# A hybrid attention layer: two attention items scored among the query products, reciprocals on GpSimd, two merge tiles among the last items, merge weights split two steps ahead

## The chip, the cores and the metric

The kernel runs on one core of one Trainium2 chip. The metric is the device time of one execution in microseconds, as a median of several runs. The engines are named as in the profile: PE is TensorE (PEld its weight loads), DVE is VectorE, ACT is ScalarE, POOL is GpSimd, and SP issues the transfers (DMAs).

## What is computed

One layer of a transformer trunk over 1024 latent tokens on a grid of 16 x 64 and 256 context tokens, width 1024: a half-step SwiGLU, two token mixers on the same normalised input, their merge, and a second half-step SwiGLU. The change lies between the projections and the merge:

```python
o_na = _neighbourhood_attention(qa, ka, va, cka, cva, rpb[l], n_rows)   # 8 heads of 64: 8 x 16 window + 256 context keys
q_mla = _mla_q(qn, _axial_rope(qr, ang_r, ang_c))                       # 8 heads of 64 + 32
o_mla = _blocked_attention(q_mla, k_mla, v_mla)                         # all 1280 keys
y = (ga * (o_na @ w_o_na) + gb * (o_mla @ w_o_mla)) @ w_out             # the merge
```

Both attentions are a softmax over the keys: scores, maximum, exponential, sum, and the product with the values divided by the sum.

## The kernel before, in words

All matrices are float32. For precision an operand is split into a high part (an ACT cast to the matmul's reduced format, `fp32r`) and a low part (a DVE subtraction); `mm3` makes three matmuls of two split operands, `weigh` two. Tiles are 128 rows high.

The order of work before the attention is written out by hand in a `Plan`: a list of main steps, with side steps set to run after given main steps by `spread`. The last steps are the products for the keys and values (`kv_heads`) and for the queries (`q_heads(0)`, `q_heads(1)`, nine steps each; the first four of these make the rotated parts, the next four the wide products). Matmuls and transfers keep the order in which they are written; transfers all go through SP's queue, which is worked in order, and a transfer waits there until its buffer is free. Stores of the plan are put off by two or three steps (`store`).

The attention is then a loop over 64 items: 32 of neighbourhood attention (8 heads, 4 column blocks `j` each) and 32 of latent attention (8 heads, 4 blocks of 256 queries). An item has three kinds of work:

- `scores`: matmuls into PSUM banks of the kind `s`; DVE takes the scores out (with the bias, in `L1840`), and finds the maximum (`L1814`, `L1847`). For a neighbourhood item this comes in two halves.
- the steps in the list `soft`: two or four exponentials with their sums on ACT (`L1849`, `L1948`), then the reciprocal of the sums on DVE (`L1851`, `L1952`), and for every second item `widen`, in which POOL spreads the reciprocals of two items over a tile (`L1806`).
- `values`: three or five parts. Each transposes a piece of the probabilities on PE, casts it (ACT) and subtracts (DVE), and returns a closure that multiplies it with the values. The last one calls `head_out`, where ACT and DVE take out the result, and POOL multiplies it by the reciprocal and writes high and low parts (`L1792` to `L1795`).

The loop runs the scores three items ahead (`AHEAD`) and the value products two parts behind (`LAG`), and spreads the next items' scores and softmax steps over the parts of the present one. Loads of a head are issued when its first item is scored: six pieces for neighbourhood attention (queries, context keys, keys; first bias; values of two blocks; context values and second bias; values of the others; third bias), in a pool `w` of 12 tiles; the third bias has a pool of its own (`y`). Before the change item 0 is scored amid the last two query products (its tiles in pool `f`); items 1 and 2 are scored, with their softmax steps right behind, between the plan and the loop.

The merge multiplies the two attention outputs (`ona`, `omla`) by two weight matrices in eight tiles `d` of 128 columns. A tile has four steps `wo_step(d, ci, s)`: two halves `ci` of the tokens, for each a product of 12 matmuls with the neighbourhood weights (`s` = 0) and one with the latent weights (`s` = 1). DVE multiplies each by its gate (`z`), adds the two and the sum is split for the output product. The weights of a tile are loaded (`wo_load`), and split in two halves (`wo_split`). The class `FirstMerge` makes the two `s` = 0 products of tile 0 ahead of time: one amid the very last item, one behind it; they use only neighbourhood results, which have long been complete.

Of the kernel before, what the change touches and what calls it, by code (L numbers as in the profile page):

```python
# [8 lines left out]
F32 = mybir.dt.float32  # L9
# [34 lines left out]
def hybrid_block(ctx: ExitStack, tc: tile.TileContext, a: dict, out: bass.AP):  # L44
# [15 lines left out]
    def open_pool(key, name, bufs, side):  # L60
        pools[key] = tc.alloc_tile_pool(name=nm(name), bufs=bufs, side=side, reuse_waits="tile")
# [1516 lines left out]
    class NaHead:  # L1578


        def loads(self, h):
            self.h = h
            i, b = h // 2, (h % 2) * 64
            self.q, self.ql, self.kvc, self.k = q, ql, kvc, k = [W() for _ in range(4)]
            for s in range(2):
                o = 64 * s
                ld(f32(q[o:o + 64, :]), qas[i][0, b:b + 64, :])
                ld(f32(ql[o:o + 64, :]), qas[i][1, b:b + 64, :])
                ld(f32(kvc[o:o + 64, 0:256]), kas[i][s, b:b + 64, NLAT:])
            yield  # L1590
            for s in range(2):
                ld(f32(k[64 * s:64 * s + 64, :]), kas[i][s, b:b + 64, :NLAT])
            self.bias = [W(F32), W(F32)]
            ld(self.bias[0][:, :768], a["bias"][h, 0])
            yield
            self.va = va = W()
            for j in range(2):
                self.values(va, j)
            yield
            ld(f32(kvc[:, 256:512]), vcs[h])  # L1600
            ld(self.bias[1][:, :768], a["bias"][h, 1])
            yield
            self.vb = vb = W()
            for j in range(2, 4):
                self.values(vb, j)
            yield
            self.bias.append(U(F32, "y"))
            ld(self.bias[2][:, :768], a["bias"][h, 2])
            yield
# [123 lines left out]
    plan.spread([lambda d=d: query_cols(0, d) for d in range(6)], o, o + 12)  # L1733
    o = len(plan.main)
    plan.step(*calls(kv_heads(1, ckv[1]), 9))
    plan.spread([lambda d=d: query_cols(1, d) for d in range(6)], o + 3, o + 14)
    plan.step(*calls(q_heads(0, cqn[0]), 9))
    o = len(plan.main)
    plan.step(*calls(q_heads(1, cqn[1]), 9))
    heads = {}  # L1740

    na0 = na_loads(0)

    def weights():
        close_pools("v")
        open_pool("w", "weights", 12, "left")
        open_pool("y", "third", 2, "left")
        open_pool("f", "first", 2, "left")

    def score_banks():  # L1750
        banks[0] = "mv"

    early = []

    def first_scores():
        if not early:
            it = na_item(0, 0)
            started.append(it)
            early.append(it.scores())
        next(early[0], None)  # L1760

    def first_soft():
        while soft:
            soft.pop(0)()

    plan.spread([weights], o - 3, o - 2)
    plan.spread(calls(na0, 6), o - 2, o + 4)
    plan.spread([score_banks], o + 2, o + 3)
    plan.spread([first_scores] * 2, o + 6, o + 8)
    plan.spread([first_soft], o + 8, o + 9)  # L1770

    ona, omla = [], []

# [34 lines left out]
    def sums_of(n):  # L1808
        if n // 2 not in sums:
            sums[n // 2] = ST(4)  # L1810
        return sums[n // 2][:, (n % 2) * 2:(n % 2) * 2 + 2]

    def copy_max(dst, src, m):
        nc.vector.tensor_scalar(dst, src, 1.0, FMIN, op0=ALU.mult, op1=ALU.max, accum_out=m)  # L1814

# [4 lines left out]
    class NaItem:  # L1820
# [3 lines left out]
        def scores(self):  # L1824
            hd, j = self.head, self.j
            kg = hd.k.rearrange("p (r c) -> p r c", c=64)
            cx = PB("s")
            key = "u" if self.n else "f"
            self.pr = pr = [U(key=key), U(key=key)]
            m, n_, l, r = ST(4), ST(2), ST(2), sums_of(self.n)  # L1830
            for s in range(2):
                loc = PB("s")
                o = s * 512 + j * P
                kw = kg[:, 4 * s:4 * s + 12, KSTART[j]:KSTART[j] + 32]
                cs = cx[:, s * 256:(s + 1) * 256]
                mmul(cs, hd.q[:, o:o + P], hd.kvc[:, 0:256], start=True, stop=False)
                mmul(cs, hd.ql[:, o:o + P], hd.kvc[:, 0:256], start=False, stop=True)
                mmul(loc[:, :384], hd.q[:, o:o + P], kw, start=True, stop=False)
                mmul(loc[:, :384], hd.ql[:, o:o + P], kw, start=False, stop=True)
                nc.vector.tensor_tensor_reduce(out=pr[s][:, :384], in0=loc[:, :384],  # L1840
                                               in1=hd.bias[BVAR[j]][:, s * 384:(s + 1) * 384], scale=1.0, scalar=FMIN,
                                               op0=ALU.add, op1=ALU.max, accum_out=m[:, 2 * s:2 * s + 1])
                if s == 0:
                    yield
            for s in range(2):
                copy_max(pr[s][:, 384:640], cx[:, s * 256:(s + 1) * 256], m[:, 2 * s + 1:2 * s + 2])
            nc.vector.tensor_reduce(n_, m.rearrange("p (s c) -> p s c", s=2), axis=AX.X, op=ALU.max, negate=True)  # L1847
            for s in range(2):
                soft.append(lambda s=s: nc.scalar.activation(pr[s][:, :640], pr[s][:, :640], AF.Exp,  # L1849
                                                             bias=n_[:, s:s + 1], accum_out=l[:, s:s + 1]))  # L1850
            soft.append(lambda: nc.vector.reciprocal(r, l))  # L1851
            if self.n % 2:
                soft.append(lambda: widen(self.n))
            yield
# [67 lines left out]
    class MlaItem:  # L1922
# [3 lines left out]
        def scores(self):  # L1926
# [21 lines left out]
                nc.scalar.activation(x, x, AF.Exp, bias=n_[:, s:s + 1], accum_out=l[:, i:i + 1])  # L1948

            def total():  # L1950
                nc.vector.tensor_tensor(r, l[:, 0:2], l[:, 2:4], op=ALU.add)
                nc.vector.reciprocal(r, r)  # L1952

            for s in range(2):
                soft.append(lambda s=s: exp(prl[s], s))
# [53 lines left out]
            for b in range(4):  # L2009
                yield lambda h=h, b=b: mla_item(h, b)  # L2010

    AHEAD = 3
    LAG = 2
    todo = list(items_())
    pending = []
# [21 lines left out]
            started.append(it)  # L2037
            yield from it.scores()

    for n in range(1, AHEAD):  # L2040
        for _ in start(n):
            pass
        while soft:
            soft.pop(0)()
    class FirstMerge:


        def load(self):
            self.r = T2()
            ld(self.r, a["wo"][0][:, 0:512])  # L2050

        def split(self):
            t = W()
            self.w = split_to(t[:, 0:512], t[:, 512:1024], self.r)
            self.pb = [PB("s") for _ in range(2)]

        def step(self, ci, ks):
            open_group[0] = True
            for k in ks:
                mm3(self.pb[ci], [x[:, k * P:(k + 1) * P] for x in self.w],  # L2060
                    [x[:, ci * 512:ci * 512 + 512] for x in ona[k]], k == 0, k == 3)
            open_group[0] = False

    fm = FirstMerge()
    for n in range(len(todo)):
        ahead = start(n + AHEAD)
        if n == len(todo) - 3:
            fm.load()
        if n == len(todo) - 2:
            fm.split()  # L2070
        parts = started[n].values()
        soft_n, soft[:] = list(soft), []
        for x, part in enumerate(parts):
            pending.append(part())
            for _ in range(-(-len(soft_n) // (len(parts) - x))):
                soft_n.pop(0)()
            for _ in range(5 // len(parts)):
                next(ahead, None)
            if n == len(todo) - 1 and x:
                fm.step(0, (x - 1,))  # L2080
            if len(pending) > LAG:
                pending.pop(0)()
        for _ in ahead:
            pass
    for w in pending:
        w()
    fm.step(1, range(4))
    pinned[0] = False

    close_pools("u", "t", "f", "y", "w")  # L2090
# [8 lines left out]
        wos[d] = [load(a["wo"][d])]  # L2099

    def wo_split(d, s):
        wos[d].append(split(wos[d][0][:, s * 512:(s + 1) * 512]))

    def z_load(d):
        for ci in range(2):
# [4 lines left out]
    def wo_step(d, ci, s):  # L2110
        c = slice(ci * 512, ci * 512 + 512)
        if ci + s == 0:
            yt.append(list(zip(*[duo() for _ in range(2)])))
        if d + s == 0:
            pb = fm.pb[ci]
        else:
            pb = PA()
            w = wos[d][1 + s]
            for k in range(4):
                mm3(pb, [x[:, k * P:(k + 1) * P] for x in w], [x[:, c] for x in (ona, omla)[s][k]], k == 0, k == 3)  # L2120
        z = zt[d, ci, s]
        vec.tensor_tensor(z, pb, z, op=ALU.mult)
        if s:
            x = zt[d, ci, 0]
            vec.tensor_tensor(x, x, z, op=ALU.add)
            hi, lo = yt[d]
            split_to(hi[ci], lo[ci], x)

    plan = Plan()
    wo_load(0)  # L2130
    z_load(0)
    wos[0].append(None)
    wo_split(0, 1)
    for d in range(KD):
        o = len(plan.main)
        plan.step(*[lambda d=d, ci=ci, s=s: wo_step(d, ci, s) for ci in range(2) for s in range(2)])
        if d + 1 < KD:
            plan.spread([lambda d=d: (wo_load(d + 1), z_load(d + 1))], o, o + 1)
            plan.spread([lambda d=d, s=s: wo_split(d + 1, s) for s in range(2)], o + 2, o + 4)
    g5row = []  # L2140
    wsets = [Set(a["wout"][e], 512, "ut"[e], "tv"[e]) for e in range(2)]
    plan.spread([lambda: wsets[0].load(0)], len(plan.main) - 8, len(plan.main) - 7)
# [182 lines left out]
```

## Time and profile before

| | us |
|---|---|
| median of three runs | 2590.11 (2586.34 to 2592.45) |
| the profiled execution | 2593.43 |
| its span | 2591.6 |
| query products of the second half of the tokens | until 1349 |
| neighbourhood attention in the loop | 1356 to 1500 |
| latent attention | 1500 to 1764 |
| merge | 1764 to 1855.5 |

The rows of the profile are read like this. A row of the timeline has its start in us from the span's beginning, its length, the engine, the line, the operation, what it writes and reads (`bm`, `bs`, `bv` are PSUM banks; `w` the tiles of heads; `xu`, `xf`, `t` working tiles; `xo` attention outputs; `d` scratch in device memory), shapes, and how many instructions it joins. In brackets stands how long the engine was idle before it, and what ended that wait. A row of the groups has the count, the busy time, the mean in ns, and the idle time before with what ended most of it. A row of the windows has a stretch, its length, the busy time of each engine with its count of instructions, the clock granted to TensorE, the share of the DMA engines' time, and GB/s. `L120`, `L132` and `L158` are helpers, through which most operations pass.

### The profile page before, as it was taken

Reading aid. Unit: us, or ns where it says so; the run is one execution under the profiler, and the core shown is the slowest. Engines: PE = TensorE matmul, PEld = TensorE weight load, DVE = VectorE, ACT = ScalarE, POOL = GpSimd, SP = SyncE. Lnnn points to the kernel's source line nnn. Section 1 sums busy time; section 2 is a strip of 40 time slices with the busy share of each in tenths; the row PEclk is TensorE's granted clock in tenths of the full one; section 3 lists DMA queues with packets and bytes.
Section 4 is the critical chain, followed back from the end, with each engine's and each line's share of the span. In section 5 each row is a group of like instructions: output and inputs, shape, how many; then the busy total and the mean of one; then the engine's idle time right before and its main releaser. Section 6 shows DMA issues by size and latency. Waiting matters only on the chain.

```text
span 2591.6 us, 38557 instructions
## 1 busy us (share of the span) xinstructions
PE 2543.2 (98%) x13289; PEld 2168.0 (84%) x13289; DVE 1884.0 (73%) x3616; ACT 1224.1 (47%) x2334; POOL 220.3 (8%) x365
## 2 busy tenths in 40 slices
PE   7999999999999999999999999999999999999998
PEld 5888888998888788889889999987788888888887
DVE  4689887877577577874559988885535788778557
ACT  4532223445445753343438887782256322323633
POOL 0000000000001100001004422220021000000002
PEclk9999999999999999999999999999999999999999
DMA  7567674877676665767888732215225566556755
GB/s 288 165 215 256 227 247 167 274 266 257 195 246 218 233 207 193 233 217 206 286 255 244 225 82 76 76 46 186 75 106 187 195 235 225 176 195 247 254 194 196
DMA packets 273892, 523.08 MB, mean 202 GB/s; under 512 B 33248, under 2 KB 84256, under 8 KB 273696
## 3 DMA queue, kind: packets, MB, share of 16 engines
q1 hardware_dynamic: 273696, 520.62, 60.1%
q8 instruction: 105, 1.72, 0.3%
q14 instruction: 91, 0.75, 0.1%
HBM read 375.21 MB, written 145.29 MB: 201 GB/s over the span
## 4 chain that ended last, share of the span: by engine, by line
PE 69%; issue 17%; DVE 6%; ACT 5%; DMA 2%; SPq 1%; POOL 0%; DVEq 0%; ACTq 0%; POOLq 0%
PE bm L158 25%; PE bs L158 25%; PE bv L158 15%; PE bm L161 2%; DVE t L120 1%; ACT xu L1948 1%; DVE xu L1814 1%; DMA w<-d 1%; PE bs L161 1%; DVE xu L120 1%; ACT t L1974 1%; ACT xu L120 1%; DVE t L1975 1%; DVE xv L120 1%; ACT t L120 1%
## 5 line engine op out<-in xcount | busy, mean ns | idle before, releaser
L158 PE MATMUL bm<-xu,xu 128*128 128x512 f32 (+1 forms) x2442 | 596.0, 388 | 3.3 <-ACT t L120 2.2
L120 ACT CAST xu<-t 128x512 fp32r<-128x512 f32 x589 | 345.5, 617 | 483.7 <-DVE t L120 329.6
L158 PEld LDWEIGHTS bm<-xu,xu 128*128 128x128 f32 x2442 | 449.9, 188 | 95.7 <-ACT t L120 4.3
L120 DVE TENSOR_TENSOR xu<-t,xu 128x512 fp32r<-128x512 f32 x589 | 382.3, 683 | 140.4 <-ACT xu L120 140.4
L158 PE MATMUL bs<-xu,xu 128*128 128x512 f32 (+2 forms) x1581 | 388.2, 384 | 0.0
L158 PE MATMUL bs<-xv,xu 128*128 128x512 f32 x1488 | 358.1, 390 | 3.1 <-DVE t L120 2.9
L158 PEld LDWEIGHTS bs<-xu,xu 128*128 128x128 f32 x1581 | 291.7, 188 | 58.0
L158 PE MATMUL bv<-xv,xu 128*128 128x512 f32 x1342 | 335.9, 389 | 0.0
L158 PEld LDWEIGHTS bs<-xv,xu 128*128 128x128 f32 x1488 | 278.5, 188 | 63.2 <-issue 5.5
L158 PEld LDWEIGHTS bv<-xv,xu 128*128 128x128 f32 x1342 | 251.5, 188 | 52.1
L120 DVE TENSOR_TENSOR xu<-xu,xu 128x512 fp32r<-128x512 f32 x291 | 195.2, 686 | 98.7 <-ACT xu L120 98.1
L120 DVE TENSOR_TENSOR t<-t,t 128x512 f32<-128x512 f32 (+3 forms) x328 | 211.0, 646 | 12.8 <-ACT t L120 9.6
L158 PE MATMUL bs<-w,w 96*128 96x512 f32 (+3 forms) x832 | 208.8, 369 | 11.1 <-DMA w<-d 5.9
L158 PE MATMUL bv<-xu,xu 128*128 128x512 f32 x722 | 191.5, 389 | 0.0
L120 POOL TENSOR_SCALAR st<-st 128x1 f32<-128x1 f32 x64 | 31.2, 487 | 1659.0 <-ACT t L120 1323.6
L120 ACT CAST xu<-xu 128x512 fp32r<-128x512 f32 x283 | 167.2, 619 | 7.5 <-POOL xo L1795 2.6
L158 PE MATMUL bm<-t,xu 128*128 128x256 f32 (+1 forms) x1272 | 160.2, 287 | 0.0
L158 PEld LDWEIGHTS bv<-xu,xu 128*128 128x128 f32 x722 | 135.4, 188 | 28.1
L158 PEld LDWEIGHTS bm<-t,xu 128*128 128x128 f32 x1272 | 156.6, 192 | 2.1
L158 PE MATMUL bv<-t,w 128*128 128x256 f32 x896 | 152.4, 291 | 2.8 <-ACT t L1974 1.7
L158 PEld LDWEIGHTS bv<-t,w 128*128 128x128 f32 x896 | 134.7, 193 | 17.3 <-DVE t L1975 4.7
L120 ACT ACTIVATE t<-t 128x512 f32<-128x512 f32 (+1 forms) x94 | 57.2, 609 | 189.8 <-DVE t L120 187.6
(217 smaller groups left out, 3207.7 us busy)
## 6 DMA issues: line engine op xcount, KB each, us to landing
d<-t SPq DMA_DIRECT2D x432, 256.0 KB, 2.6
t<-d SPq DMA_DIRECT2D x348, 256.0 KB, 4.9
xu<-in_f1w SPq DMA_DIRECT2D x106, 512.0 KB, 4.7
xu<-in_f2w SPq DMA_DIRECT2D x58, 512.0 KB, 4.6
t<-in_wada SPq DMA_DIRECT2D x112, 256.0 KB, 4.8
w<-d SPq DMA_DIRECT2D x112, 256.0 KB, 4.6
t<-in_f1w SPq DMA_DIRECT2D x77, 256.0 KB, 5.3
t<-in_f2w SPq DMA_DIRECT2D x77, 256.0 KB, 5.2
```

What stands on the lines that cost most here:

```text
L120: return lambda *x, **y: pin(f(*x, **y))
L158: return pin(nc.tensor.matmul(o, s, m, start=start, stop=stop, skip_group_check=open_group[0]))
L161: return pin(nc.tensor.transpose(o, x, i))
L1814: nc.vector.tensor_scalar(dst, src, 1.0, FMIN, op0=ALU.mult, op1=ALU.max, accum_out=m)
L1948: nc.scalar.activation(x, x, AF.Exp, bias=n_[:, s:s + 1], accum_out=l[:, i:i + 1])
L1974: nc.scalar.copy(t[0], pb)
L1975: nc.vector.tensor_tensor(t[1], pb, f32(t[0]), op=ALU.subtract)
```

## The change

Four things. First, items 0 and 1 are scored in four halves behind the query steps 4 to 7 of `q_heads(1)`, and their softmax steps run behind steps 6 and 7; items 2 and 3 are scored inside item 0 of the loop. For this the head's loads and the pools come one step earlier, the second bias is loaded with the first, pool `f` has two tiles of 1280 columns, and pool `y` one tile. Second, the reciprocals are taken by POOL: a power of -1/2 and a square; in latent attention the sum of the two partial sums goes to POOL too. Third, `FirstMerge` makes the `s` = 0 products of tiles 0 and 1 in 16 steps of three matmuls: one with each part of the last three items from the second part on, one behind each of the two value products left over, and the rest after that. Fourth, a merge tile's weights are loaded two tiles ahead and split in the first two steps of the tile before, instead of the last two.

```diff
-            ld(self.bias[0][:, :768], a["bias"][h, 0])
+            for v in range(2):
+                ld(self.bias[v][:, :768], a["bias"][h, v])
...
-            ld(self.bias[1][:, :768], a["bias"][h, 1])
...
-    plan.spread([lambda d=d: query_cols(1, d) for d in range(6)], o + 3, o + 14)
+    plan.spread([lambda d=d: query_cols(1, d) for d in range(6)], o + 3, o + 13)
...
-        open_pool("y", "third", 2, "left")
-        open_pool("f", "first", 2, "left")
+        open_pool("y", "third", 1, "left")
+        open_pool("f", "first", EARLY, "left")
...
-    plan.spread([weights], o - 3, o - 2)
-    plan.spread(calls(na0, 6), o - 2, o + 4)
+    plan.spread([weights], o - 4, o - 3)
+    plan.spread(calls(na0, 6), o - 3, o + 4)
     plan.spread([score_banks], o + 2, o + 3)
-    plan.spread([first_scores] * 2, o + 6, o + 8)
-    plan.spread([first_soft], o + 8, o + 9)
+    plan.spread([lambda j=j: first_scores(j) for j in (0, 0, 1, 1)], o + 4, o + 8)
+    plan.spread([first_soft] * 2, o + 6, o + 9)
...
+    def inverse(r, l):
+        nc.gpsimd.tensor_tensor(r, l, mhalf, op=ALU.pow)
+        nc.gpsimd.tensor_tensor(r, r, r, op=ALU.mult)
...
-            soft.append(lambda: nc.vector.reciprocal(r, l))
+            soft.append(lambda: inverse(r, l))
...
-                nc.vector.tensor_tensor(r, l[:, 0:2], l[:, 2:4], op=ALU.add)
-                nc.vector.reciprocal(r, r)
+                nc.gpsimd.tensor_tensor(r, l[:, 0:2], l[:, 2:4], op=ALU.add)
+                inverse(r, r)
...
-    for n in range(1, AHEAD):
-        for _ in start(n):
-            pass
-        while soft:
-            soft.pop(0)()
     class FirstMerge:
+        def __init__(self):
+            self.pb, self.w = {}, {}
+            self.todo = [(d, ci, k) for d in range(2) for ci in range(2) for k in range(4)]
...
+        def step(self):
+            if not self.todo:
+                return
+            d, ci, k = self.todo.pop(0)
+            if k == 0:
+                self.pb[d, ci] = PB("m" if d + ci == 2 else "s")
             open_group[0] = True
-            for k in ks:
-                mm3(self.pb[ci], [x[:, k * P:(k + 1) * P] for x in self.w],
-                    [x[:, ci * 512:ci * 512 + 512] for x in ona[k]], k == 0, k == 3)
+            mm3(self.pb[d, ci], [x[:, k * P:(k + 1) * P] for x in self.w[d]],
+                [x[:, ci * 512:ci * 512 + 512] for x in ona[k]], k == 0, k == 3)
...
-        ahead = start(n + AHEAD)
-        if n == len(todo) - 3:
-            fm.load()
-        if n == len(todo) - 2:
-            fm.split()
+        ahead = chain(*[start(x) for x in (range(EARLY, AHEAD + 1) if n == 0 else (n + AHEAD,))])
+        for d in range(2):
+            if n == len(todo) - 6 + d:
+                fm.load(d)
+            if n == len(todo) - 5 + d:
+                fm.split(d)
...
-            if n == len(todo) - 1 and x:
-                fm.step(0, (x - 1,))
+            if n >= len(todo) - 3 and (n, x) != (len(todo) - 3, 0) and len(fm.todo) > 4:
+                fm.step()
...
     for w in pending:
         w()
-    fm.step(1, range(4))
+        fm.step()
+    while fm.todo:
+        fm.step()
...
-        if d + s == 0:
-            pb = fm.pb[ci]
+        if s == 0 and d < 2:
+            pb = fm.pb[d, ci]
...
         if d + 1 < KD:
-            plan.spread([lambda d=d: (wo_load(d + 1), z_load(d + 1))], o, o + 1)
-            plan.spread([lambda d=d, s=s: wo_split(d + 1, s) for s in range(2)], o + 2, o + 4)
+            plan.spread([lambda d=d, s=s: wo_split(d + 1, s) for s in range(2)], o, o + 2)
+        if d + 2 < KD:
+            plan.spread([lambda d=d: (wo_load(d + 2), z_load(d + 2))], o + 1, o + 2)
```

More of the change, by code (lines that the diff above doesn't have):

```diff
@@ L1740, in hybrid_block @@
     heads = {}
+    EARLY, AHEAD = 2, 3
     na0 = na_loads(0)
@@ L1753, in hybrid_block, with first_scores @@
     early = []
-    def first_scores():
-        if not early:
-            it = na_item(0, 0)
+    def first_scores(j):
+        if len(early) == j:
+            it = na_item(0, j)
             started.append(it)
             early.append(it.scores())
-        next(early[0], None)
+        next(early[j], None)
     def first_soft():
@@ L1827, in scores @@
             cx = PB("s")
-            key = "u" if self.n else "f"
-            self.pr = pr = [U(key=key), U(key=key)]
+            if self.n < EARLY:
+                t = pools["f"].tile([P, 1280], F32, tag="f", name=nm("xf"))
+                self.pr = pr = [t[:, 0:640], t[:, 640:1280]]
+            else:
+                self.pr = pr = [U(), U()]
             m, n_, l, r = ST(4), ST(2), ST(2), sums_of(self.n)
@@ L2010, in items_ @@
                 yield lambda h=h, b=b: mla_item(h, b)
-    AHEAD = 3
     LAG = 2
@@ L2038, in start, with load, split @@
             yield from it.scores()
-    for n in range(1, AHEAD):
-        for _ in start(n):
-            pass
-        while soft:
-            soft.pop(0)()
     class FirstMerge:
-        def load(self):
+        def __init__(self):
+            self.pb, self.w = {}, {}
+            self.todo = [(d, ci, k) for d in range(2) for ci in range(2) for k in range(4)]
+        def load(self, d):
             self.r = T2()
-            ld(self.r, a["wo"][0][:, 0:512])
-        def split(self):
+            ld(self.r, a["wo"][d][:, 0:512])
+        def split(self, d):
             t = W()
-            self.w = split_to(t[:, 0:512], t[:, 512:1024], self.r)
-            self.pb = [PB("s") for _ in range(2)]
-        def step(self, ci, ks):
+            self.w[d] = split_to(t[:, 0:512], t[:, 512:1024], self.r)
+        def step(self):
[4 more added lines that the diff above has]
+                self.pb[d, ci] = PB("m" if d + ci == 2 else "s")
             open_group[0] = True
-            for k in ks:
-                mm3(self.pb[ci], [x[:, k * P:(k + 1) * P] for x in self.w],
-                    [x[:, ci * 512:ci * 512 + 512] for x in ona[k]], k == 0, k == 3)
+            mm3(self.pb[d, ci], [x[:, k * P:(k + 1) * P] for x in self.w[d]],
+                [x[:, ci * 512:ci * 512 + 512] for x in ona[k]], k == 0, k == 3)
             open_group[0] = False
@@ L2101, in wo_split @@
     def wo_split(d, s):
-        wos[d].append(split(wos[d][0][:, s * 512:(s + 1) * 512]))
+        wos[d].append(None if s == 0 and d < 2 else split(wos[d][0][:, s * 512:(s + 1) * 512]))
     def z_load(d):
@@ L2129, in hybrid_block @@
     plan = Plan()
[L2130 to L2133, printed above, removed]
+    for d in range(2):
+        wo_load(d)
+        z_load(d)
+    for s in range(2):
+        wo_split(0, s)
     for d in range(KD):
```

## The prediction

> **What bounds the kernel.** I read the page first, then the windows view for the places that the change touches, then the timeline and the list of waits inside them.
>
> ```profile
> span 2591.6 us, 38557 instructions
> PE 2543.2 (98%) x13289; PEld 2168.0 (84%) x13289; DVE 1884.0 (73%) x3616; ACT 1224.1 (47%) x2334; POOL 220.3 (8%) x365
> PE 69%; issue 17%; DVE 6%; ACT 5%; DMA 2%; SPq 1%; POOL 0%; DVEq 0%; ACTq 0%; POOLq 0%
> ```
>
> TensorE is the bound nearly everywhere, so time can come only from holes in PE or from stretches at a lowered clock. The windows (length; busy PE, PEld, DVE, ACT, POOL; granted clock, DMA share, GB/s) show where those are:
>
> ```profile
> 1340.00:1350.00 10.00, 9.94 (x50) 8.24 (x48) 4.74 (x10) 2.36 (x5) 0.64 (x4) 1.00 0.57 210
> 1354.30:1357.70 3.40, 3.36 (x13) 3.27 (x14) 3.15 (x17) 1.74 (x4) 0.00 (x0) 0.50 1.00 210
> 1364.50:1367.90 3.40, 3.40 (x18) 3.40 (x17) 2.45 (x10) 1.65 (x6) 0.40 (x1) 0.50 1.05 366
> 1390.00:1490.00 100.00, 94.41 (x737) 91.80 (x736) 92.29 (x334) 88.58 (x213) 49.09 (x84) 1.00 0.81 232
> 1500.00:1735.00 235.00, 234.47 (x1673) 216.97 (x1671) 199.82 (x597) 188.64 (x425) 59.75 (x102) 1.00 0.26 68
> 1739.40:1764.00 24.60, 22.38 (x147) 20.60 (x146) 14.67 (x30) 14.95 (x32) 6.49 (x11) 0.86 0.22 76
> 1746.80:1753.60 6.80, 6.50 (x28) 6.20 (x29) 4.66 (x9) 4.21 (x10) 2.65 (x5) 0.50 0.02 7
> 1764.00:1855.50 91.50, 89.36 (x373) 68.37 (x373) 53.31 (x82) 20.23 (x36) 1.86 (x3) 1.00 0.45 158
> ```
>
> Row 4 is neighbourhood attention at its steady pace: PE, DVE and ACT are all around nine tenths busy. An item is 31 matmuls (8 scores, 10 transposes, 12 value products, one for the sums on average), so 737 in 100 us are 23.8 items of 4.2 us. Row 5 is latent attention: PE leaves 0.53 us of 235 idle, so a shorter DVE or a busier POOL (25%) moves nothing there. Rows 6 to 8 are the last three items and the merge; two stretches at the start and one at the end run at half clock.
>
> **1. Two items scored amid the query products.**
>
> ```profile
> 1316.78 1.32 SPq L132 DMA_DIRECT2D w<-d  x2
> 1344.15 0.84 PE L158 MATMUL bs<-w,w 128*128 128x256 f32 x4
> 1344.83 4.29 PE L158 MATMUL bv<-xu,xu 128*128 128x512 f32 x18
> 1350.51 1.28 ACT L1849 ACT_TABLE_LOAD   x1
> 1351.29 0.32 SPq L132 DMA_DIRECT2D d<-t  x1
> 1351.66 5.45 SPq L132 DMA_DIRECT2D w<-d  x8
> 1353.60 0.17 DVE L1851 RECIPROCAL st<-st 128x2 f32<-128x2 f32 x1 [1.80 <-ACT xf L1849]
> 1354.34 2.55 PE L158 MATMUL bs<-w,w 128*128 128x256 f32 x8 [2.05 <-DVE st L1840]
> 1363.10 0.60 PE L158 MATMUL bs<-w,w 128*128 128x384 f32 x2 [1.82 <-DMA w<-d]
> ```
>
> Today the exponential's table is loaded after the last query product, DVE stands behind the reciprocal, and PE waits 2.05 us. With two items scored and their exponentials taken amid the queries, that chain is covered (row 1: ACT 2.4 and DVE 4.7 us of 10); if the cover failed it would come back whole. What is late next: the eight loads of head 1 are issued at 1351.66 on SP's queue, right behind the last store of the queries (1351.29), and the last of them, k, holds PE until 1363.10. The change leaves them behind that store. It also puts three halves of a scoring ahead of the last product where one stood; a half costs 1344.83 - 1344.15 = 0.68 us. So store, loads and k come 2 x 0.68 = 1.4 us later, about 1364.5, and PE has done by then the very work that it has done now at 1363.10. The hole moves from 1352 to 1359-1364 and does not close. In exchange ACT and DVE have nothing in arrears at that point, which I put at 1.4 us over the next items: sum **0**. Bounds: -7.3 if the landing doesn't bind (waits of 2.05 and 1.82, and half of the two 3.4 us stretches at half clock); +3.1 if the arrears give nothing and one more stretch runs at half clock (1.4 + 1.7).
>
> Head 0's loads go one step earlier, past stores of the first queries; its k is issued at 1316.78 now, and the first scoring moves from 1344 to about 1335, so even at the 11.4 us that head 1's loads take there is room. The second bias is loaded ahead of the values, and the third has one buffer instead of two: its load is the last of a head, and behind it on SP's queue stand only loads for four items later. 0 each; without that slack, one load's issue, about 0.5 us a head.
>
> **2. Reciprocals by GpSimd.** In 1366 to 1490 us (28 items; the waits of PE on the second row: total, times, longest):
>
> ```profile
> L1851 DVE RECIPROCAL st<-st 128x2 f32<-128x2 f32 x28 | 4.4, 157 | 4.6 <-ACT xu L1849 4.5
> PE bs L158 <- DMA w<-d: 4.1, 5, 1.2
> 1392.28 1.45 SPq L132 DMA_DIRECT2D w<-d  x2
> 1397.61 0.59 PE L158 MATMUL bs<-w,w 128*128 128x384 f32 x2 [1.17 <-DMA w<-d]
> ```
>
> DVE is rid of 4.4 us of work and of 4.6 us in which it stood for ACT's sums: 9.0 us at most. PE cannot take all of it. Once a head, k of the next head is issued when the bias buffer of the present one comes free (1392.28) and lands 5.3 us later (1397.61). That part of a head's 16.8 us doesn't shrink; only about 2.5 of 4 items run at DVE's pace. 9.0 x 2.5/4 = 5.6; PE's own holes in 124 us are 124 x (1 - 0.944) = 6.9. ACT and PE are nearly as full as DVE, so I take half: **-3**. Bounds 0 (all goes into waits for k) and -6. In latent attention 32 reciprocals and 32 adds leave DVE: 0 by row 5 of the windows, -1 at best.
>
> What POOL pays, by the form view:
>
> ```profile
> L120 POOL TENSOR_TENSOR st<-st,mhalf 128x1 f32<-128x1 f32 x64 | 54.1, 845 | 5.3
> L120 POOL TENSOR_TENSOR st<-st,mhalf 128x8 f32<-128x8 f32 x1 | 2.1, 2083 | 298.0 <-DVE st L120 298.0
> L1795 POOL TENSOR_TENSOR xo<-t,xo 64x256 fp32r<-64x256 f32 x64 | 46.9, 732 | 5.1
> ```
>
> No row has a power over two columns. Between 845 ns for one and 2083 ns for eight a straight line gives 1.02 us; the square lies under 0.73, I take 0.3. POOL is busy 0.49 x 4.2 = 2.06 us an item and goes to 3.4 of 4.2. Behind the waiting power on its queue stand the head outputs, whose results are read only in the merge, and the widened sums, read more than an item later: 0.
>
> [...]
>
> **3. Two merge tiles amid the last items.** The timeline:
>
> ```profile
> 1746.96 1.74 PE L158 MATMUL bv<-t,w 128*128 128x256 f32 x4 [1.10 <-ACT t L1974]
> 1754.90 0.72 PE L158 MATMUL bv<-t,w 128*128 128x256 f32 x4
> 1755.81 0.72 PE L158 MATMUL bv<-t,w 128*128 128x256 f32 x4
> 1763.95 2.91 PE L158 MATMUL bs<-xo,w 128*128 128x512 f32 x12
> 1767.09 0.62 ACT L120 CAST xu<-xu 128x512 fp32r<-128x512 f32 x1 [2.58 <-POOL xo L1795]
> 1767.76 3.33 PE L158 MATMUL bm<-xo,xu 128*128 128x512 f32 x12 [0.91 <-ACT xu L120]
> 1786.39 2.88 PE L158 MATMUL bm<-xo,xu 128*128 128x512 f32 x12
> 1789.24 3.37 PE L158 MATMUL bs<-xo,xu 128*128 128x512 f32 x12
> 1792.44 2.88 PE L158 MATMUL bm<-xo,xu 128*128 128x512 f32 x12
> 1846.85 3.38 PE L158 MATMUL bs<-xo,xu 128*128 128x512 f32 x12
> 1852.78 2.88 PE L158 MATMUL bs<-xo,xu 128*128 128x512 f32 x12
> 1855.50 5.81 PE L158 MATMUL bm<-xu,xu 128*128 128x512 f32 x24
> ```
>
> A part of an item takes PE 0.91 us when nothing holds it (1754.90 to 1755.81); a merge product of 12 matmuls 2.72 (1852.78 to 1855.50). The last three items hold 15 parts = 13.7 us, one merge product = 2.7, and some 1.4 of left-over products: 17.8. They take 1739.4 to 1763.95 = 24.5. So 6.7 us are lost: no scoring is left to fill PE while ACT does the last exponentials, and the clock is halved for 6.8 us (3.3 of the loss). The change puts three products (8.2 us) there. The work of the second tile only moves; the holes fill and the clock should hold. ACT is busy 14.95 of these 24.6 us, most of it early, so I keep a quarter of the loss (1.7) and take -5. The second tile's load, cast (0.62) and subtraction lie in latent attention, where ACT and DVE have 15 to 20% free: 0, or 1.3 uncovered.
>
> Behind the last item one product's filling (2.72) becomes three steps of 0.68, while the first product still waits for a split that stands behind POOL (1767.09): +0.7.
>
> **4. Merge weights split two steps ahead.** Today each tile's second weight half is split just before its use: 1786.39 to 1792.44 is 6.05 for two products of 2.72, so 0.61 lost, and the same on to the one begun at 1846.85, six in all: 3.7. The splits now stand two products earlier, behind nothing late: -3.7. The first turn of this kind (tile 1) loses 1.7 today, of which I keep 0.6 because tile 1's own split comes only one product ahead: -1.1. The extra weight and four gate tiles held fit the pools, and SP runs ahead of the steps anyway: 0.
>
> End together: -5 + 0.7 - 3.7 - 1.1 = -9.1. The split that waits for POOL leaves PE idle 1.8 us, more than the 1.10 at 1746.96 before the halved stretch, so a halved stretch (+1.7) is about as likely as not; I count a third of it: **-8.5**. Bounds: all that is lost, 6.7 + 7.2 (91.55 us for 31 products of 2.72) = -13.9; and -2, if the holes only move.
>
> [...]
>
> **The sum.** 0 - 3 - 8.5 = -11.5 us. The profiled execution took 2593.4 (span 2591.6 and 1.8 around it); the median is 2590.1, 0.13% lower. 2590.1 - 11.5 = 2578.6, said as 2579.
>
> **Rivals.** A, the start gains too: the loads of head 1 land in time. For it speaks that head 0's transfers are gone earlier; against it, 11.4 us from issue to use today with nothing else on the queue. -5 there: 2574. B, POOL becomes the bound of neighbourhood attention: with 2.08 for the power (the eight-column row) and 0.73 for the square an item takes POOL 4.87 against 4.2, 32 x 0.67 = 21 us slower: -8.5 + 21 = +13, 2603. It decides from 4.2 - 2.06 = 2.14 us for the two instructions; the one-column row speaks against it. C, head switches swallow part 2: the wait for k grows by what DVE saves; the 4.1 us of such waits speak for it: -8.5, 2582. D, the change does little: the last exponentials still hold PE, the clock still falls, and the start loses 3: about -3, 2587.
>
> **Chances.** My forecast 0.50, A 0.12, C 0.18, D 0.13, B 0.07. A difference under 0.2% (5.2 us) cannot be told from none here. Forecast, A and C are faster: 0.80; D is the same: 0.13; B slower: 0.07. Leaving out B and half of D, the range is 2571 (end -12, others -7) to 2588.
>
> **What would show it.** Right: clock 1.00 in the last three items, merge products evenly 2.72 apart, no DVE reciprocal, POOL near 0.8 busy in neighbourhood attention, and PE still waiting for k of head 1 near 1364. Wrong: that wait gone (A), POOL full (B), longer PE waits on loads (C), 0.50 left at the end (D).

## The result, and the profile after

The changed kernel takes 2594.11 us (median of 11 runs, 2591.86 to 2596.65) against 2589.18 for the kernel before in the same session: a ratio of 1.0019 [1.001, 1.0028]. It is 5 us slower, where 11.5 us less had been forecast, and outside the range. The profiled execution took 2594.11, with this on its page:

```profile
span 2592.3 us, 38694 instructions
PE 2543.5 (98%) x13289; PEld 2167.0 (84%) x13289; DVE 1880.2 (73%) x3520; ACT 1223.0 (47%) x2334; POOL 276.3 (11%) x525
```

The totals hardly move: POOL has 160 instructions and 56 us more, DVE 96 instructions fewer. The windows view (columns as before) puts the change stage by stage:

```profile
1340.00:1350.00 10.00, 10.00 (x53) 8.49 (x52) 5.47 (x14) 4.97 (x10) 0.90 (x2) 1.00 0.57 210
1354.50:1357.90 3.40, 3.40 (x14) 3.06 (x14) 2.24 (x12) 0.05 (x1) 1.87 (x7) 0.50 1.05 212
1361.30:1368.20 6.90, 6.10 (x26) 6.13 (x27) 2.42 (x9) 2.22 (x6) 1.35 (x4) 0.51 1.01 358
1390.00:1490.00 100.00, 96.98 (x761) 94.94 (x760) 93.54 (x317) 91.38 (x220) 70.63 (x134) 1.00 0.84 236
1500.00:1735.00 235.00, 228.03 (x1579) 204.66 (x1577) 185.88 (x503) 177.01 (x399) 81.74 (x175) 1.00 0.26 68
1752.20:1776.20 24.00, 23.23 (x159) 20.75 (x158) 12.73 (x22) 14.30 (x30) 7.88 (x15) 1.00 0.01 1
```

Row 4, neighbourhood attention: 761 matmuls in 100 us instead of 737, a gain. Row 6, the last items: full clock and PE 97% busy, a gain. Row 5, latent attention: 1579 matmuls in 235 us where there were 1673, with DVE, ACT and the weight loads all less busy than before and only POOL busier (82 against 60 us). That stage lost what the others won.

The profiled execution of the kernel before was a long one (2593.43 against a median of 2589.18), so the spans of the two profiles differ by only 0.7 us where the medians differ by 4.9.

To follow this over all kernels I cut each profiled execution at starts of PE rows that every version has: the last matmul of the last product of the queries (128x512, `bv<-xu,xu`), and the transposes `bv<-ident,rope` of the sums, which come once for every two items (a pair; there are 32). For the changed kernel the second, sixteenth and thirtieth pair and the first product of the output weights are

```profile
1374.95 0.38 PE L161 MATMUL bv<-ident,rope 128*128 128x128 f32 x2
1492.06 0.38 PE L161 MATMUL bv<-ident,rope 128*128 128x128 f32 x2
1735.49 0.38 PE L161 MATMUL bv<-ident,rope 128*128 128x128 f32 x2
1856.14 0.61 PE L158 MATMUL bm<-xu,xu 128*128 128x512 f32 x2
```

The same rows of the kernel before begin at 1374.70, 1495.74, 1726.11 and 1855.50. The differences, for these two kernels and those of the experiments (times are the medians; the kernel before took 2589.2 to 2590.9 beside them):

| kernel | time | queries to pair 2 | pairs 2 to 16, neighbourhood | pairs 16 to 30, latent | pair 30 to output |
|---|---|---|---|---|---|
| before | 2590 | 26.0 | 121.0 | 230.4 | 129.4 |
| changed | 2594.1 | 26.2 | 117.1 | **243.4** | 120.7 |
| changed, latent reciprocals on DVE | 2580.9 | 25.4 | 117.9 | 230.5 | 119.5 |
| changed, all reciprocals on DVE | 2583.7 | 26.1 | 120.3 | 230.6 | 119.5 |
| changed, 15 working tiles | 2575.5 | 25.1 | 118.2 | 227.7 | 117.2 |
| changed, POOL in written order | 2578.2 | 24.7 | 118.2 | 228.9 | 119.1 |
| before + latent reciprocals on POOL | 2603.0 | 24.6 | 120.5 | **243.4** | 127.4 |
| before + part 1 | 2593.2 | 25.6 | 120.6 | 230.5 | 126.8 |
| before + part 4 | 2582.5 | 24.6 | 121.0 | 230.5 | 120.8 |
| before + parts 3 and 4 | 2580.2 | 24.5 | 121.3 | 230.6 | 118.4 |
| before + neighbourhood reciprocals on POOL | 2589.1 | 25.9 | 118.2 | 230.4 | 128.2 |
| before + 15 working tiles | 2589.7 | 26.0 | 120.6 | 230.4 | 126.5 |
| 15 tiles, head 1 early | 2573.0 | 22.9 | 117.8 | 227.7 | 116.7 |
| 15 tiles, head 1 early, written order | 2574.5 | 24.3 | 117.5 | 227.7 | 117.3 |

What comes behind the last column is 736.1 to 736.5 in all of them. Of the first two rows the differences are +0.2, -3.9, +13.0 and -8.7: together +0.6, where the spans differ by 0.7. Two cautions. In the kernels with part 1, two halves of a scoring (1.3 us) that the first column held before lie ahead of it, so there it is not like with like. And the 129.4 of the kernel before are the longest end of their kind: the four others with neither part 3 nor part 4 take 126.5 to 128.2.

**Where the 13 us arise.** The list of waits between 1560 and 1720 us (total, times, longest), of the changed kernel:

```profile
POOL st L1959 <- ACT t L1956: 52.2, 9, 5.9
ACT t L1982 <- POOL xo L1796: 13.7, 9, 1.7
PEld bv L158 <- DVE t L1983: 8.9, 18, 0.5
DVE t L1983 <- POOL xo L1796: 8.0, 9, 1.1
PEld bv L158 <- ACT t L1982: 5.6, 12, 0.8
ACT t L1982 <- POOL t L1793: 5.3, 9, 0.6
```

`L1982` and `L1983` are the cast and the subtraction that split the probabilities for the value products; nothing in their data comes from POOL. They wait for a working tile `t` to write into: one that a head output releases with its last step (`L1796`), or the one that it hands from the first item of a pair to the second, which is free after `L1793`. In the kernel before neither waited for POOL at all, and PE's weights waited only this much:

```profile
PEld bv L158 <- DVE t L1975: 3.2, 10, 0.5
```

The timeline of one such place in the changed kernel:

```profile
1605.35 0.41 DVE L1792 TENSOR_TENSOR t<-t,bv 64x256 f32<-64x256 f32 x1
1606.50 0.19 POOL L1959 TENSOR_TENSOR st<-st 128x2 f32<-128x2 f32 x1 [5.87 <-ACT t L1956]
1606.65 0.73 POOL L1793 TENSOR_TENSOR t<-t,t 64x256 f32<-64x256 f32 x1
1607.34 0.69 POOL L1815 TENSOR_TENSOR st<-st,mhalf 128x2 f32<-128x2 f32 x1
1607.99 0.40 POOL L1795 CAST xo<-t 64x256 fp32r<-64x256 f32 x1
1608.34 0.19 POOL L1816 TENSOR_TENSOR st<-st 128x2 f32<-128x2 f32 x1
1608.49 0.74 POOL L1796 TENSOR_TENSOR xo<-t,xo 64x256 fp32r<-64x256 f32 x1
1609.26 0.59 ACT L1982 CAST t<-bm 128x512 fp32r<-128x512 f32 x1 [1.27 <-POOL xo L1796]
1609.74 1.15 ACT L1956 ACTIVATE xu<-xu,st 128x1024 f32<-128x1024 f32 x1
```

At 1605.76 DVE has finished the tile of a head output. POOL could begin (`L1793`), but at the head of its queue stands the new sum of another item (`L1959`), which waits for ACT's last exponential until 1606.50. Then the three steps of the head output (`L1793`, `L1795`, `L1796`) alternate with the sum, the power and the square. The tile that they read is free at 1609.23, 3.5 us after DVE wrote it; the cast starts at 1609.26, and the next exponential stands behind it on ACT. With the sums on DVE (the third kernel of the table) the same three steps run without a break, 2.0 us in all:

```profile
1602.30 0.41 DVE L1792 TENSOR_TENSOR t<-t,bv 64x256 f32<-64x256 f32 x1
1602.86 0.74 POOL L1793 TENSOR_TENSOR t<-t,t 64x256 f32<-64x256 f32 x1 [5.30 <-DVE t L1792]
1603.66 0.39 POOL L1795 CAST xo<-t 64x256 fp32r<-64x256 f32 x1
1604.13 0.73 POOL L1796 TENSOR_TENSOR xo<-t,xo 64x256 fp32r<-64x256 f32 x1
```

There the tile is free at 1604.86, 2.15 us after DVE wrote it (1602.71), against 3.47 in the changed kernel: 1.3 us later. Of these, 0.74 pass before the first step begins, and 0.58 go to the power and the square that stand between the three steps. The 1.3 us appear as the cast's wait of 1.27 here. Over the 14 pairs the stage loses 13.0 / 14 = 0.93 a pair.

### The profile page after: what moved, and what is told of

The parts are those of the page before. It is cut to its first block, busy times and chain, and to the rows that moved or that the text cites. A ratio compares the mean times of both kernels' runs of the same rounds, so it can differ in the third digit from the quotient of the medians.

```text
span 2592.3 us, 38694 instructions
## 1 busy us (share of the span) xinstructions
PE 2543.5 (98%) x13289; PEld 2167.0 (84%) x13289; DVE 1880.2 (73%) x3520; ACT 1223.0 (47%) x2334; POOL 276.3 (11%) x525
```

## The experiments

The theory: a waiting POOL instruction makes head outputs release their working tiles late, and the pool of 12 has none to spare. The main rival: POOL's added work is simply too much, or something else in the change slows latent attention.

**Undo the latent reciprocals.** On the changed kernel:

```diff
-                nc.gpsimd.tensor_tensor(r, l[:, 0:2], l[:, 2:4], op=ALU.add)
-                inverse(r, r)
+                nc.vector.tensor_tensor(r, l[:, 0:2], l[:, 2:4], op=ALU.add)
+                nc.vector.reciprocal(r, r)
```

> The changed kernel with the sum and the reciprocal of latent attention back on DVE (neighbourhood attention keeps POOL). Theory: the 15 us that latent attention lost (17.9 us for two items where it took 16.6) come from POOL's new instructions there alone; so two items take 16.6 again and the time is about 2579, 10 below the kernel before. Rival: the loss comes from the other edits (pools, one buffer for the third bias, weights held for the merge); then it stays at 17.9 and 2594.

Measured: 2580.89 us (2579.37 to 2585.21), ratio 0.9972 [0.9961, 0.9983]. Latent attention is back at 230.5, and with it 13 us. What is left of the change gains 9.0 us against the 2589.9 beside it.

**Undo all reciprocals.** In addition:

```diff
-            soft.append(lambda: inverse(r, l))
+            soft.append(lambda: nc.vector.reciprocal(r, l))
```

> The changed kernel with all reciprocals back on DVE. If POOL's reciprocals gained the 3.6 us seen in neighbourhood attention, this is 3 to 4 us above the previous run, about 2583, and a head of four items there takes 16.7 us again instead of 16.1. Rival: those 3.6 us come from the loads' new order; then both runs are equal.

Measured: 2583.74, ratio 0.9978 [0.9969, 0.9986]; the neighbourhood stage goes from 117.9 to 120.3. So in that stage POOL's reciprocals are worth having.

**The latent reciprocals alone.** On the kernel before:

```diff
+    def inverse(r, l):
+        nc.gpsimd.tensor_tensor(r, l, mhalf, op=ALU.pow)
+        nc.gpsimd.tensor_tensor(r, r, r, op=ALU.mult)
...
-                nc.vector.tensor_tensor(r, l[:, 0:2], l[:, 2:4], op=ALU.add)
-                nc.vector.reciprocal(r, r)
+                nc.gpsimd.tensor_tensor(r, l[:, 0:2], l[:, 2:4], op=ALU.add)
+                inverse(r, r)
```

> The kernel before with only the sum and the reciprocal of latent attention moved to POOL. Theory: 14 to 16 us slower, about 2604, with 17.9 us for two items. Rival (the edit harms only together with the others): 2589.

Measured: 2602.95, ratio 1.0057 [1.0044, 1.0071], 13 us slower with nothing else changed (14 to 16 expected). Its waits in latent attention are those of the changed kernel, line for line shifted:

```profile
ACT t L1978 <- POOL xo L1795: 13.7, 9, 1.7
DVE t L1979 <- POOL xo L1795: 8.0, 9, 1.1
ACT t L1978 <- POOL t L1792: 5.3, 9, 0.6
```

**More tiles, the same order.** On the changed kernel:

```diff
-    open_pool("t", "half", 12, "right")
+    open_pool("t", "half", 15, "right")
```

> The changed kernel with 15 working tiles of 512 columns in the attention instead of 12, nothing else. Theory: in latent attention POOL's sum waits for ACT's exponentials, the head output queued behind it on POOL reads a working tile, and ACT's casts and DVE's subtractions wait for that tile. With three more tiles these waits (27 us in 160 now) fall under 8 and the time is 2579 to 2583. [...]

Measured: 2575.53 (2573.88 to 2576.22), ratio 0.995 [0.9937, 0.9962]. All of POOL's work is still there and in the same mixed order, and POOL's own wait for ACT too, yet nobody waits for POOL and PE's weights wait for nothing:

```profile
POOL st L1959 <- ACT t L1956: 48.5, 10, 5.2
ACT t L1982 <- PE bm L161: 18.7, 25, 1.0
```

So POOL is not too slow; the lateness costs only when no other tile is free. The time is below the 2579 to 2583 of the theory; the kernel before with 15 tiles, further down, shows where the rest comes from.

**The same tiles, another order.** On the changed kernel, POOL's instructions of an item in the order in which they are written, so that a head output's three steps stand together ahead of the next sum:

```diff
-        nc.gpsimd.tensor_tensor(o, o, rb, op=ALU.mult)
+        pool.tensor_tensor(o, o, rb, op=ALU.mult)
...
-        nc.gpsimd.tensor_tensor(r, l, mhalf, op=ALU.pow)
+        pool.tensor_tensor(r, l, mhalf, op=ALU.pow)
```

and so for the head output's cast and subtraction, the square, the sum and `widen`; `pool` keeps the written order.

> The changed kernel, with 12 working tiles as it has, but GpSimd's instructions of an item keep the order in which they are written: the head output's three (multiply, copy, subtract) stand together and never behind a sum that still waits for ACT's exponentials. Theory (the working tile that a head output reads comes free late because it stands behind the waiting sum): two latent items take 16.6 us again instead of 17.8, 16 pairs by 1.1 = -15 to -18 us against the changed kernel, total 2577 to 2582; PE's and ACT's waits for GpSimd in latent attention go from about 27 us to under 5. Rival (GpSimd is simply too slow for its added work, whatever the order): stays at 2592 to 2596. A middle result (2584 to 2590) would say that the power itself, 0.7 us on the queue, delays the release as well.

Measured: 2578.21, ratio 0.9951 [0.9938, 0.9963]. With 12 tiles and all of POOL's work, what remains of the casts' waits for POOL and of the weights' waits is

```profile
ACT t L1982 <- POOL st L120: 2.3, 3, 0.9
PEld bv L158 <- DVE t L1983: 1.5, 5, 0.4
```

Either cure alone brings the 13 us back, and both undo the same waits: the loss takes the order and the short pool together. Both cures go beyond the level of before: 227.7 and 228.9 against 230.4.

**Were tiles short before the change?** The kernel before with 15 tiles.

> The kernel before with 15 working tiles instead of 12, nothing else. Theory (the supply of working tiles was already a little short before the change: its pairs of latent items take 16.6 to 16.8 where 15 tiles gave an even 16.4 after it): 13 pairs by 0.25 = -3, total 2586 to 2588. Rival 1 (tiles were not short before; the change alone made them so): 2589 to 2592. Rival 2 (more tiles are worth much by themselves, so that the gain seen with 15 tiles is not the repair of the change's fault): 2580 or less.

Measured: 2589.69, ratio 0.9995 [0.9987, 1.0004]; latent attention 230.4 as before. My theory of a shortage before the change falls, rival 1 holds. The 2.7 us below 230.4 come neither from the tiles alone (230.4) nor from the other parts of the change (230.5 with the latent reciprocals on DVE). They come when both hold, enough tiles and a DVE that is rid of sums and reciprocals: with 15 tiles the 3.2 us for which PE's weights waited for its subtraction (`L1975`) are gone.

**The end, in two steps.** On the kernel before, part 4 alone, and parts 3 and 4 (the hunks of the diff above for `wo_load`, `wo_split` and `FirstMerge`).

> The kernel before with part 4 alone (the merge weights split two steps ahead). By the prediction's terms: -3.7 - 1.1 = -4.8, total 2585 to 2587, of part 3 then remain the other 6 of the 10.7 that the two parts gave together. Rival (the splits are late only because the first tile is, and part 3 brings all): 2589 or more.

> The kernel before with parts 3 and 4 alone (two merge tiles amid the last items, splits two steps ahead). Theory: the end is worth what the landmarks gave in the changed kernel, 9 to 11 us: 2579 to 2581, half clock gone at the end. Rival (the gain at the end came only because the latent items before it were slowed, so that transfers and splits had more time): 2586 or more.

Measured: 2582.52, ratio 0.9973 [0.9963, 0.9983], and 2580.21, ratio 0.9959 [0.9946, 0.9971]. The splits bring 7.6 us of the 10.7, the two merge tiles 2 to 3. The 2582.52 lie below the 2585 to 2587 expected, so the split term was too small.

**The start alone.** On the kernel before, part 1.

> The kernel before with part 1 alone (items 0 and 1 scored amid the query products). Theory: the hole moves from the exponential's chain to the wait for the keys of head 1 and the time stays: 2588 to 2592. Rival (the start is worth the two waits of 2 us, which the slower middle hid in the changed kernel): 2583 to 2586.

Measured: 2593.15 (2590.41 to 2594.25, 11 runs), ratio 1.0009 [1.0001, 1.0018]: 2.3 us slower, by the interval 0.3 to 4.7, and above the 2588 to 2592 expected. Its first column is 25.6 against 26.0, but two halves of a scoring now lie ahead of that column. Where the loss arises is shown with the prediction's part 1 below.

**The neighbourhood reciprocals alone.** On the kernel before, `inverse` for the neighbourhood items only.

> The kernel before with the reciprocals of the neighbourhood items alone on GpSimd. By the prediction's term: -3 (0 to -6), total 2586 to 2588. If the parts add up: the changed kernel's +5 less the end's -10.7, the start's +2 and the latent reciprocals' +12 to +13 leaves +1 to -0; the rival is therefore 2590 to 2592.

Measured: 2589.12, ratio 0.9997 [0.9988, 1.0006]. By the time alone this is neither -3 nor clearly 0; the interval holds -3. The stage is clearer: 118.2 against 121.0. Over all profiled executions the seven kernels with these reciprocals on DVE take 120.3 to 121.3 (mean 120.8) and the seven with POOL 117.1 to 118.2 (mean 117.8): -2.9, and no overlap.

**What is left at the start.** 15 tiles, and the keys and queries of head 1 issued two steps earlier:

```diff
+    na1 = na_loads(1)
...
+    plan.spread(calls(na1, 2), o + 4, o + 6)
```

with a further `yield` in `loads`, so that its first two pieces can stand alone.

> The changed kernel with 15 working tiles, and the first two of the pieces of head 1 (queries, context keys, keys) issued at the query steps 4 and 5, ahead of the last stores of the queries. Theory (what is left at the start is the wait for the keys of head 1, issued behind the last store): the two waits of 1.78 us for transfers go, and with them the second half-clock stretch: -3.5 to -5 against 15 tiles alone, about 2571. Rival 1 (the earlier loads take bandwidth or buffers from the query products): 0 or a loss, 2575 to 2579. Rival 2 (the hole moves on to the next late piece): 0 to -2.

Measured: 2572.99, ratio 0.9929 [0.9915, 0.9942], the fastest here. Against 15 tiles alone the first stage goes from 25.1 to 22.9. Both waits for transfers are gone from PE's timeline, and a new one stands in their place:

```profile
1355.85 1.10 PE L158 MATMUL bs<-w,w 128*128 128x256 f32 x4 [1.39 <-DVE st L1851]
1363.75 0.41 DVE L1795 TENSOR_TENSOR t<-t,bv 64x256 f32<-64x256 f32 x1 [1.84 <-ACT t L1794]
1365.25 0.55 DVE L1851 CUSTOM_DVE_ANT_0 xu<-bs,w 128x384 f32<-128x384 f32 x1
1365.86 1.49 PE L158 MATMUL bs<-w,w 128*128 128x256 f32 x4 [3.23 <-DVE st L1851]
```

The scoring of head 1 now waits for scores that DVE takes out late (`L1851`, the former `L1848`), since DVE stands behind a head output (`L1795`) that waits for ACT. The gain is 2.5 us between the medians, 3.5 with each taken against the kernel before of its own session (2589.9 and 2590.9): at the near end of the theory (-3.5 to -5) or just short of it, and above rival 2 (0 to -2). Of the 2.2 us that the profile shows in the first stage, about 1.4 are not safe, an estimate from the next kernel: with the same early loads it takes 24.3 there, against 22.9 here, where one half-clock stretch of 3.4 us is left (granted clock 0.89 from 1363 to 1366 us and 0.77 from 1366 to 1372).

**All repairs together**, with POOL in written order as well.

> The changed kernel with all three repairs: 15 working tiles, GpSimd's item instructions in written order, head 1's first pieces two steps earlier. Theory (order and tiles cure the same wait, so they don't add): as with 15 tiles and head 1 early, 2572 to 2575. Rival (the order saves something of its own, since results come earlier): 2568 to 2571.

Measured: 2574.49, ratio 0.9938 [0.9926, 0.9951]. This is within the theory's 2572 to 2575. Order and tiles don't add: they cure the same wait.

## Why the prediction was wrong

**What held, and what held in part.** *Part 1*, in part: a hole stands at the wait for k, as foretold, but the stage grew by 1.5 us where 0 had been forecast. Both kernels hold the same work from the query product ahead of the first early scoring on. It begins, in the kernel before and in the changed one, at

```profile
1331.05 4.27 PE L158 MATMUL bm<-xu,xu 128*128 128x512 f32 x18
1329.84 4.27 PE L158 MATMUL bm<-xu,xu 128*128 128x512 f32 x18
```

and pair 2 comes 43.65 us behind it before and 45.11 after. In the profiles of the six kernels without part 1 this takes 42.1 to 43.7 (mean 42.9), in the six with it and with head 1's loads in their old place 43.6 to 45.1 (mean 44.4). So the 1.4 us that DVE and ACT were to give back over the next items are not seen. The result is inside the bounds stated for this term (up to +3.1). The timeline after shows the loads behind the last store as foretold and k at 1362.10, but also two waits for transfers where one stood, and PE still waiting 1.39 us for DVE:

```profile
1350.53 1.09 SPq L132 DMA_DIRECT2D d<-t  x2
1351.67 4.95 SPq L132 DMA_DIRECT2D w<-d  x8
1353.90 1.38 PE L158 MATMUL bs<-w,w 128*128 128x256 f32 x4 [1.39 <-DVE st L1848]
1359.84 0.48 PE L158 MATMUL bs<-w,w 128*128 128x256 f32 x2 [1.78 <-DMA w<-d]
1362.10 0.98 PE L158 MATMUL bs<-w,w 128*128 128x384 f32 x2 [1.78 <-DMA w<-d]
```

*Part 2 in neighbourhood attention*: -3 forecast, -2.9 measured. POOL goes to 0.71 busy, not 0.8: by the form view the power costs 0.70 us (1.02 estimated), the square 0.19 (0.3).

```profile
L1815 POOL TENSOR_TENSOR st<-st,mhalf 128x2 f32<-128x2 f32 x29 | 20.2, 696 | 1.6 <-ACT xu L1857 0.4
L1816 POOL TENSOR_TENSOR st<-st 128x2 f32<-128x2 f32 x29 | 5.6, 194 | 2.3
```

Rival B, which needed 2.14 for the two, is out. So is rival C: PE's waits for loads did not grow (in 1366 to 1490 us, against 4.1 before):

```profile
PE bs L158 <- DMA w<-d: 2.1, 3, 1.0
```

*The end*: -8.5 forecast, -8.7 between the two profiles, -10.7 in the medians of parts 3 and 4 alone. That the first two agree is in part luck. Against the mean of the five profiles with neither part 3 nor part 4 (127.7) the changed kernel gains 7.0. The first merge product behind the items (1778.70) does not wait for a split behind POOL, for which +0.7 had been counted. The merge products start 2.72 apart but for two turns, 3.55 and 3.12. There the second tile's split is late, behind a transfer of its weights that was issued only at 1778.79; "SP runs ahead of the steps anyway" did not hold for this tile:

```profile
1778.70 2.94 PE L158 MATMUL bm<-xo,xu 128*128 128x512 f32 x12
1781.47 2.88 PE L158 MATMUL bs<-xo,xu 128*128 128x512 f32 x12
1784.35 0.62 ACT L120 CAST xu<-xu 128x512 fp32r<-128x512 f32 x1 [0.53 <-DMA xu<-in_wo]
1785.02 3.29 PE L158 MATMUL bm<-xo,xu 128*128 128x512 f32 x12 [0.67 <-ACT xu L120]
1788.14 2.88 PE L158 MATMUL bs<-xo,xu 128*128 128x512 f32 x12
1790.86 2.88 PE L158 MATMUL bm<-xo,xu 128*128 128x512 f32 x12
```

Its two terms were not the right size: the splits bring 7.6 (stated 4.8), the merge tiles 2 to 3 (stated 4.3). With part 4 alone the merge from its first product to the output weights takes 85.7 us (1759.37 to 1845.03) instead of 91.55, so 5.9 of the 7.6 is in the merge itself. Part of what I charged to the last items, the half clock of 6.8 us, was particular to the execution that I read (below).

**The step that failed** is the sentence on POOL's queue: "Behind the waiting power on its queue stand the head outputs, whose results are read only in the merge, and the widened sums, read more than an item later: 0." It named the right queue and the right neighbours, and asked who reads their *results*. It did not ask who waits for what they *read*: a head output holds a working tile until its last step, and ACT and DVE write the next probabilities into tiles of that pool. In place of 0 this measured +13.0 (0.93 us a pair), and nothing in my range or rivals covered it, since rival B had POOL as a bound by amount, in the other attention. Neighbourhood attention takes the power and the square on POOL without harm: between 1366 and 1490 us the list of waits has no cast and no subtraction that waits for POOL. No run shows why the two attentions differ in this.

A second, smaller miss hides under it. I put the relief of DVE in latent attention at "0 by row 5 of the windows, -1 at best", since PE stood idle for 0.53 us of 235. It is -2.7 once tiles suffice. The window with 15 tiles shows why the idle time was the wrong thing to read:

```profile
1500.00:1735.00 235.00, 235.00 (x1692) 219.82 (x1691) 203.05 (x547) 193.71 (x431) 87.86 (x188) 1.00 0.27 71
```

1692 matmuls against 1673 in the same 235 us, though PE was "busy" for 234.47 of them before. A row of a value product is 0.28 us long on average here, while the next begins 0.12 us after it (median) when the two follow each other, so a delay of up to 0.16 us leaves no idle time between the rows. The count of matmuls tells it, the busy share doesn't.

Without the one fault the change gives -9.0 (2580.9, inside the range); with the fault cured, 2575.5. Stage by stage the change comes to +1.5 at the start (0 forecast), -2.9 in neighbourhood attention (-3), +13.0 in latent attention (0) and -7.0 at the end (-8.5). Together this is +4.6, where the medians differ by 4.9. The first two of these are differences between the means of the kernels with and without the part, the last one is taken from the mean without parts 3 and 4.

## What to carry to other kernels

When an instruction that waits is put on an engine with time to spare, look at every instruction behind it twice: who needs what it writes, and who needs the buffer that it reads. A queue with two thirds of its time free (POOL was busy for 81.7 of 235 us) can still hold a tile 1.3 us longer, and in a pool without slack that is charged to the engines that allocate from it. A wait of an engine for a producer whose data it doesn't use is the sign of it (ACT's casts here, 13.7 us behind `L1796`); more buffers (three here) or another order on the queue tell it from an engine that is too slow. And in a stage that looks full, count the matmuls per microsecond (1692 against 1673 in 235 us here) instead of trusting the busy share.

## What the runs showed of the hardware

By the means, the cost of a power on GpSimd does not lie on a line over the columns: 845 ns for 128x1 in the kernel before (64 of them in another place, under a helper; their median 550, the longest 5016), 696 for 128x2 in the changed kernel and 2083 for 128x8. A line through the first and the last overestimated the second by half (1.02 us); from the median of the first it would have given 0.77.

The half clock is not settled by the wait alone. In four profiles without part 3 PE has the same wait in the last items: 1.10 us in the kernel before, 1.12 with 15 tiles, 1.09 with neighbourhood reciprocals on POOL, 1.10 with part 4. In the first three a half-clock stretch of 6.8, 3.4 and 3.4 us begins at its end or within 1 us of it (four transposes take 1.05 us in it and 0.60 outside); in the fourth there is none (granted clock 1.00 from 1740 to 1760 us). Between 1300 and 1870 us the stretches are 3.4, 3.4 and 6.8 us long in the kernel before, 3.4 and 6.8 in the changed one. No run shows why the same wait sometimes costs and sometimes doesn't. I had counted a third of a stretch for a longer wait at the end; that wait did not come (0.67 us stand elsewhere), and no stretch either (1.00 from 1368.3 to 1870 us).
